# One encoder layer on one NeuronCore: the windowed-attention scores taken two tiles at a time, their low-part product on 64 rows

## The chip, the cores and the metric

The kernel runs on one core of one Trainium2 chip. The metric is the device time of one execution in microseconds (us); where several runs are shown, their median. The engines have short names below: PE is the matrix engine (TensorE), PEld its weight loads, DVE VectorE, ACT ScalarE, POOL GpSimd, and SP the engine that issues the transfers (DMAs).

## The reference, cut to what matters

The layer takes x (2048 tokens, 1024 features) through a LayerNorm, one input projection, three mixers side by side (spatial gating, a depthwise convolution, windowed attention), one output projection, and a last LayerNorm of `alpha*x + y`. The change touches the attention only:

```
s = einsum(q, kb) * HEAD_DIM**-0.5          # 8 query heads of 64, 2 key heads, 4 query heads share one
s = where(|key - query| <= 128, s + bias, -1e30)
m = max(max(s), sink);  p = exp(s - m);  p = p / (sum(p) + exp(sink - m))
o = einsum(p, vb)
```

Everything is computed in float32 quality. PE takes the type fp32r, which keeps fewer bits, so each operand is split into a high part (a rounded copy) and a low part (what the rounding lost), and a product is the sum of partial products of the parts.

## The kernel before, in words

**Stages.** First the input LayerNorm, the transposes of x and the projections of values and keys (to about 130 us). Then 72 steps of the input projection, `feat` (lines 134 to 142): 16 weight blocks in four token chunks of 512 (two more blocks, the last attention gates, make steps 64 to 71), each step 24 matmuls of 512 columns. Beside them run the spatial gating, the convolution on DVE (62 passes over 2048 columns, line 451, spread over steps 8 to 47) and its LayerNorm. From step 67 on the attention is mixed in, and after the last step it runs alone to the end.

**Queries.** Steps 32 to 47 are of kind `cq`. `evac` (line 522) hands the product in PSUM to `split_store` (line 269), which makes the high part on ACT (line 276, with the scale -1/8), the low part on DVE (line 277), and stores them to two DRAM tensors, `qh_d` and `ql_d`. `split_store` serves the keys too (line 290). On DVE the passes of the convolution that belong to a step are tied behind its line 277 through `last[0]` (line 922).

**Keys.** `load_k` (line 561) puts four tiles in SBUF: high and low part of each of the two key heads, each one twice, in partitions 0 to 63 and again in 64 to 127.

**Blocks and slots.** The attention goes by 16 blocks of 128 tokens. `slot(i, h)` (line 816), h from 0 to 7, does a piece of three blocks at once: scores of block i, the probabilities' transposes and value products of block i-1, the output projection of block i-2. On PE the order inside a slot is: the score tile (`scores`, line 686), four transposes (`ptrans`, line 725, in slots 0 to 5 of an inner block), two value matmuls (`pv`, line 735, in slots 2 to 7), six matmuls of the output projection (`oproj`, line 761). Each engine works its instructions in order; the order is set by a scheduler at build time, which follows the program except where it sees an engine waiting.

**One score tile.** At a block's start the query parts are read back into one tile, high part in partitions 0 to 63, low part in 64 to 127 (lines 656, 657), and ACT copies them into `q` with the tokens regrouped (line 660): tile h holds one key head's four query heads for 32 of the 128 tokens, which makes 128 columns. Its window is 288 keys. Two matmuls of 128 rows fill it:

```
for e in range(2):
    T.matmul(ps[:, 0:n], d["q"][:, h, :],
             kt[e * 2 + kv][:, g0:g0 + n], start=(e == 0), stop=(e == 1))
```

The first (e = 0) sums high query times high key and low query times high key; the second high query times low key and low query times low key. DVE then takes the tile out of PSUM, adds the bias and finds the row's extreme (line 697). PSUM tiles of the tag `psD`, of which there are two, hold the scores, and in the projection steps also every other step's `feat` product. In slots 3 and 7 `softmax` (line 702) does the exponentials on ACT (line 710) and the normalisation on POOL (line 719). `finish` (line 796) ends a block with a LayerNorm: POOL's power (line 107), DVE's line 809, two POOL passes.

Of the kernel before, what the change touches and what calls it, by code (L numbers as in the profile page):

```python
# [7 lines left out]
F32 = mybir.dt.float32  # L8
F32R = mybir.dt.float32r
AF = mybir.ActivationFunctionType  # L10
ALU = mybir.AluOpType
# [3 lines left out]
P = 128  # L15
SEQ = 2048
# [3 lines left out]
CH = 512  # L20
# [7 lines left out]
NH = 8  # L28
HD = 64
QS = 32  # L30
WK = 2 * P + QS
# [24 lines left out]
def trunk_kernel(  # L56
# [5 lines left out]
    V, S, G, T, SY = nc.vector, nc.scalar, nc.gpsimd, nc.tensor, nc.sync  # L62
# [4 lines left out]
    def f32(ap):  # L67
        return ap.bitcast(F32)

    constp = tc.alloc_tile_pool(name="constp", bufs=1)  # L70
    dram = tc.alloc_tile_pool(name="dramp", bufs=1, space=DRAM)
# [3 lines left out]
    spo_d = dram.tile([SEQ, 256], F32, name="spo_d")  # L75
    yh_d = dram.tile([4, P, SEQ], F32, name="yh_d")
    yl_d = dram.tile([4, P, SEQ], F32, name="yl_d")
    qh_d = dram.tile([NH * HD, SEQ], F32, name="qh_d")
    ql_d = dram.tile([NH * HD, SEQ], F32, name="ql_d")
    kh_d = dram.tile([P, SEQ], F32, name="kh_d")  # L80
    kl_d = dram.tile([P, SEQ], F32, name="kl_d")
    v_d = dram.tile([NT, P, 2, 2, HD], F32, name="v_d")
# [15 lines left out]
    p_ln = tc.alloc_tile_pool(name="p_ln", bufs=2, side="right", reuse_waits="tile")  # L98
    psp = tc.alloc_tile_pool(name="psp", bufs=2, space=PSUM)
# [46 lines left out]
    last = [None]  # L146
# [29 lines left out]
    for hf in range(2):  # L176
        for a, dst in ((0, grow), (1, brow)):
            ps = psp.tile([P, CH], F32, tag=("psD", "psE")[a], name=f"row{a}_{hf}")
# [87 lines left out]
        V.tensor_tensor(out=vt[:, :, 1, :], in0=src, in1=f32(vt[:, :, 0, :]), op=ALU.subtract)  # L266
        SY.dma_start(v_d[t].rearrange("p a l d -> p (a l d)"), f32(vt).rearrange("p a l d -> p (a l d)"))

    def split_store(ps, hd, ld, scale, pool, bufs, n=CH):
        hi = pool.tile([P, n], F32R, tag="shi", name="shi", bufs=bufs)  # L270
        lo = pool.tile([P, n], F32R, tag="slo", name="slo", bufs=bufs)
        if scale is None:
            S.copy(hi, ps)
            V.tensor_tensor(out=lo, in0=ps, in1=f32(hi), op=ALU.subtract)
        else:
            S.activation(hi, ps, AF.Copy, scale=scale)
            last[0] = V.scalar_tensor_tensor(out=lo, in0=ps, scalar=scale, in1=f32(hi),
                                             op0=ALU.mult, op1=ALU.subtract).ins
        SY.dma_start(hd, f32(hi))
        SY.dma_start(ld, f32(lo))  # L280

    def keys(c, o, n):
        ps = psp.tile([P, n], F32, tag="psD", name=f"ck{c}_{o}")
        for k in range(NK):
            T.matmul(ps, ckh[:, k, :], xc[c][:, 0, k, o:o + n], start=(k == 0), stop=False)
            T.matmul(ps, ckh[:, k, :], xc[c][:, 1, k, o:o + n], start=False, stop=False)
        for k in range(NK):
            T.matmul(ps, ckl[:, k, :], xc[c][:, 0, k, o:o + n], start=False, stop=(k == NK - 1))
        ts = slice(c * CH + o, c * CH + o + n)
        split_store(ps, kh_d[:, ts], kl_d[:, ts], None, p_ln, 1, n)  # L290

    plan = [(BB, "bb", 0), (BA, "ba", 0), (BB + P, "bb", 1), (BA + P, "ba", 1),
            (AU, "au", 0), (AG, "ag", 0), (AU + P, "au", 1), (AG + P, "ag", 1)]
# [13 lines left out]
    for t in range(NT + LOOK):  # L307
# [26 lines left out]
        if u == 4:  # L334
            keys(0, 256, 256)
# [6 lines left out]
    pm = tc.alloc_tile_pool(name="pm", bufs=2, side="right", reuse_waits="tile")  # L342
# [179 lines left out]
    def evac(kind, a, c, ps):  # L522
        cs = slice(c * CH, (c + 1) * CH)
        ps_cs = slice(PAD + c * CH, PAD + (c + 1) * CH)
        if kind == "bb":
            if c == 0:
                g_ = pm.tile([P, SEQ + 2 * PAD + 2], F32, tag="glu", name=f"glu{a}")
                V.memset(g_[:, 0:PAD], 0.0)
                V.memset(g_[:, PAD + SEQ:SEQ + 2 * PAD], 0.0)
                glu.append(g_)  # L530
            S.activation(glu[a][:, ps_cs], ps, AF.Sigmoid)
        elif kind == "ba":
            last[0] = V.tensor_tensor(out=glu[a][:, ps_cs], in0=ps, in1=glu[a][:, ps_cs], op=ALU.mult).ins
            if c == NC - 1:
                avail[0] += KW
        elif kind == "au":
            tm = pm.tile([P, CH], F32, tag="tmp", name=f"gu{a}_{c}")
            S.activation(tm, ps, AF.Gelu_apprx_tanh)
            pt = spt.pop((a, c))
            last[0] = V.tensor_tensor(out=tm, in0=pt, in1=tm, op=ALU.mult).ins  # L540
            ug[a, c] = tm
        elif kind == "cq":
            fs = slice(a * P, (a + 1) * P)
            split_store(ps, qh_d[fs, cs], ql_d[fs, cs], -(HD ** -0.5), pm, 2)
        else:
            tm = pm.tile([P, CH], F32, tag="tmp", name=f"{kind}{a}_{c}")
            S.activation(tm, ps, AF.Silu)  # L547
            if kind == "ag":
                up = ug.pop((a, c))
                last[0] = V.tensor_tensor(out=up, in0=tm, in1=up, op=ALU.mult).ins  # L550
                store_y(a, c, up)
            elif kind == "bg":
                G.tensor_tensor(out=tm, in0=tm, in1=ybt[a][:, cs], op=ALU.mult)
                store_y(2 + a, c, tm)
            else:
                SY.dma_start(g_d[a * P:(a + 1) * P, cs], tm)


    kt = []
# [9 lines left out]
    ar = {}  # L569
    sink = constp.tile([P, NH], F32, name="sink")  # L570
    nsink = constp.tile([P, NH], F32, name="nsink")
# [72 lines left out]
    def load_v(i):  # L644
        SY.dma_start(f32(ar["v"][i % 8]), v_d[i].rearrange("p a l d -> p a (l d)"))

    def rng(i):
        return max(i - 1, 0), min(i + 2, NT)
# [4 lines left out]
    def start_block(i):  # L653
        raw = ar["q"][i % 2]
        cs = slice(i * P, (i + 1) * P)
        SY.dma_start(raw[0:HD], qh_d.rearrange("(h d) t -> d h t", d=HD)[:, :, cs])
        SY.dma_start(raw[HD:P], ql_d.rearrange("(h d) t -> d h t", d=HD)[:, :, cs])
        q = wsp.tile([P, NH, P], F32R, tag="whi", name=f"q{i}")
        for kv in range(2):
            S.copy(q[:, kv * 4:kv * 4 + 4, :].rearrange("p j (r t) -> p j r t", t=QS),  # L660
                   raw[:, kv * 4:kv * 4 + 4, :].rearrange("p r (j t) -> p j r t", t=QS))
        d = {"q": q, "p": [], "pt": {}}
        for nm in "egl":
            d[nm] = pm.tile([P, NH], F32, tag="sm" + nm, name=f"sm{nm}{i}")
        st[i] = d
# [15 lines left out]
    def window(i, j):  # L681

        return (max(QS * j, P) if i == 0 else QS * j,
                min(QS * j + WK, 2 * P) if i == NT - 1 else QS * j + WK)

    def scores(i, h):
        d = st[i]
        kv, j = h // 4, h % 4
        k0, k1 = window(i, j)
        n, b0 = k1 - k0, k0 - QS * j  # L690
        g0 = (i - 1) * P + k0
        ps = psp.tile([P, WK], F32, tag="psD", name=f"s{i}_{h}")
        for e in range(2):
            T.matmul(ps[:, 0:n], d["q"][:, h, :],  # L694
                     kt[e * 2 + kv][:, g0:g0 + n], start=(e == 0), stop=(e == 1))
        s = ar["s"][(i * 2 + kv) % 3 * 4 + j]
        V.tensor_tensor_reduce(out=s[:, k0:k1], in0=ps[:, 0:n], in1=ar["bias"][:, kv, b0:b0 + n],  # L697
                               scale=1.0, scalar=nsink[:, h:h + 1], op0=ALU.add, op1=ALU.min,
                               accum_out=d["g"][:, h:h + 1])
        d["p"].append(s)  # L700

    def softmax(i, kv):
        d = st[i]
# [112 lines left out]
    def slot(i, h):  # L816


        a, b, c = i, i - 1, i - 2
        if h == 0:  # L820
            if a < NT:
                start_block(a)
                if a >= 1 and a + 1 < NT:
                    load_v(a + 1)
            if 0 <= b < NT:
                load_mix(b)
        groups = []
        if 0 <= b < NT:
            lo, hi = rng(b)
            groups = [(kv, j) for kv in range(2) for j in range(hi - lo)]  # L830
        if a < NT:
            scores(a, h)
            if h % 4 == 3:
                softmax(a, h // 4)
        if h < len(groups):
            ptrans(b, *groups[h])
        if 2 <= h < len(groups) + 2:
            pv(b, *groups[h - 2])
        if c == 0:
            oproj(0, 0, h)  # L840
        if c == 1 and h < 2:
            for k in range(4 * h, 4 * h + 4):
                oproj(0, 1, k)
            if h == 1:
                finish(0)
        if c == NT - 1:
            if h < 4:
                oproj(c, 0, 2 * h)
                oproj(c, 0, 2 * h + 1)
            elif h % 2 == 0:  # L850
                oproj_last(c, h // 2 - 2)
        elif 0 < c < NT:
            hf, k = (h // 2) % 2, (h // 4) * 4 + (h % 2) * 2
            oproj(c, hf, k)
            oproj(c, hf, k + 1)
        if h == NH - 1:
            if 0 <= b < NT:
                gate(b)
            if 0 < c < NT:
                finish(c)  # L860
# [33 lines left out]
    for s, (n, c) in enumerate(steps):  # L894
# [16 lines left out]
        ps = feat(wts[n], c, f"{n}_{c}", tag="psE" if s > 11 and kind != "bg" and s % 2 else "psD")  # L911
# [66 lines left out]
```

## Time and profile before

| | |
|---|---|
| Median of 3 runs | 864.47 us (861.98 to 865.37) |
| The profiled execution: its time / its span | 863.25 us / 861.4 us |
| Busy share of PE, PEld, DVE, ACT, POOL | 96%, 82%, 67%, 41%, 31% |
| Granted PE clock, mean | 0.994 |

A timeline row reads: start in us, duration in us, engine, line, operation, output and inputs by the program's names, rows x columns, how many in a row; in brackets the idle time of that engine in front of it and what ended it. Matmuls are pipelined: one's recorded duration (0.39 us at 512 columns) is longer than its turn on the engine, so turns are read from one start to the next. In the chain of waits each piece has only the time that it adds to the chain.

### The profile page before, as it was taken

To read this page: it belongs to the slowest core of one execution; us is meant where nothing else is said; L and a number is where in the kernel's file an instruction comes from. 1 tells how busy PE (TensorE), PEld (TensorE's weight loads), DVE (VectorE), ACT (ScalarE), POOL (GpSimd) and SP (SyncE) were. 2 spreads that over 40 slices of the span, in tenths; PEclk is the share of its full clock that TensorE was granted. 3 is DMA by queue.
4 is the path that set the end of the run, shared out by engine and by line. 5 is a ranking of instruction groups with operands and counts; after the bars stand their busy time and mean duration, and the time that the engine had idled before them with its cause. 6 is when DMAs were issued, how large, how long until landed. Compare 5 with 4: busy or idle time off the path is not lost.

```text
span 861.4 us, 11898 instructions
## 1 busy us (share of the span) xinstructions
PE 830.8 (96%) x4156; PEld 705.6 (82%) x4156; DVE 574.9 (67%) x1012; ACT 352.3 (41%) x764; POOL 270.8 (31%) x320
## 2 busy tenths in 40 slices
PE   6899999999999999999899999999999999999996
PEld 6799987778888888888688887887888888888875
DVE  4888912575779888989642102676788877777764
ACT  3544321332144341122223214865555656565540
POOL 1332410330000000001233320115566655666654
PEclk9999999999999999999999999999999999999999
DMA  8577433232122224378755668987544554442221
GB/s 292 175 242 245 175 130 93 87 98 86 37 74 98 85 74 138 125 250 258 240 188 146 194 189 197 297 309 161 153 116 117 142 150 131 116 117 86 86 95 53
DMA packets 115800, 130.19 MB, mean 151 GB/s; under 512 B 8868, under 2 KB 87251, under 8 KB 115196
## 3 DMA queue, kind: packets, MB, share of 16 engines
q1 hardware_dynamic: 115740, 129.43, 48.9%
q8 instruction: 33, 0.54, 0.3%
q14 instruction: 27, 0.22, 0.1%
HBM read 74.86 MB, written 55.07 MB: 151 GB/s over the span
## 4 chain that ended last, share of the span: by engine, by line
PE 74%; DVE 8%; POOL 6%; DMA 4%; issue 3%; ACT 2%; SPq 1%; POOLq 0%; DVEq 0%; ACTq 0%
PE ft L139 13%; PE ft L140 13%; PE ft L141 13%; PE out L772 4%; PE out L773 4%; PE out L774 4%; PE pt L727 3%; PE s L694 3%; PE av L255 3%; PE av L256 3%; PE av L258 2%; PE pv L744 2%; PE pv L745 2%; POOL arena L719 2%; PE xT L242 2%
## 5 line engine op out<-in xcount | busy, mean ns | idle before, releaser
L139 PE MATMUL ft<-xc,hi_f 128*128 128x512 f32 x576 | 226.5, 393 | 0.0
L141 PE MATMUL ft<-xc,lo_f 128*128 128x512 f32 x576 | 224.5, 390 | 0.0
L140 PE MATMUL ft<-xc,hi_f 128*128 128x512 f32 x576 | 224.4, 390 | 0.0
L451 DVE SCALAR_TENSOR_TENSOR acc<-glu,cw,acc 128x2048 f32<-128x2048 f32 x60 | 140.8, 2346 | 0.6
L141 PEld LDWEIGHTS ft<-xc,lo_f 128*128 128x128 f32 x576 | 108.1, 188 | 22.6
L139 PEld LDWEIGHTS ft<-xc,hi_f 128*128 128x128 f32 x576 | 108.2, 188 | 22.1 <-ACT so L436 0.2
L140 PEld LDWEIGHTS ft<-xc,hi_f 128*128 128x128 f32 x576 | 108.2, 188 | 21.5
L131 POOL TENSOR_TENSOR lo_f<-raw_f,hi_f 128x1024 fp32r<-128x1024 f32 x8 | 21.3, 2659 | 239.5 <-ACT hi_f L129 229.7
L710 ACT ACTIVATE arena<-arena,smg 128x288 f32<-128x288 f32 (+4 forms) x128 | 67.5, 528 | 56.7 <-DVE smg L697 55.6
L697 DVE CUSTOM_DVE_ANT_0 arena<-s,arena,nsink 128x288 f32<-128x288 f32 (+4 forms) x128 | 62.7, 492 | 37.8 <-DMA arena<-qh_d 19.3
L732 DVE TENSOR_TENSOR arena<-pt,arena 128x512 fp32r<-128x512 f32 x92 | 62.8, 685 | 14.8 <-ACT arena L731 14.6
L731 ACT CAST arena<-pt 128x512 fp32r<-128x512 f32 x92 | 53.2, 582 | 33.0 <-PE pt L727 32.4
L727 PE MATMUL pt<-ident,arena 128*128 128x128 f32 x368 | 56.1, 274 | 4.9 <-DVE arena L732 4.9
L757 POOL TENSOR_TENSOR arena<-arena,gt 128x512 f32<-128x512 f32 x16 | 20.7, 1296 | 121.0 <-DVE arena L750 73.2
L694 PEld LDWEIGHTS s<-k,q 128*128 128x128 f32 x256 | 46.8, 188 | 12.9 <-DVE smg L697 1.5
L694 PE MATMUL s<-k,q 128*128 128x288 f32 (+4 forms) x256 | 54.5, 297 | 1.3 <-ACT cg L547 0.7
L719 POOL TENSOR_SCALAR arena<-arena,sml 128x288 f32<-128x288 f32 (+2 forms) x104 | 50.1, 500 | 6.3 <-ACT bot L748 3.9
L772 PE MATMUL out<-wo,yh 128*128 128x512 f32 x124 | 52.0, 419 | 0.0
L727 PEld LDWEIGHTS pt<-ident,arena 128*128 128x128 f32 x368 | 44.1, 140 | 8.7 <-issue 4.4
L773 PE MATMUL out<-wo,yh 128*128 128x512 f32 x124 | 49.3, 397 | 0.0
L774 PE MATMUL out<-wo,yl 128*128 128x512 f32 x124 | 48.8, 394 | 0.0
L772 PE MATMUL out<-wo,arena 128*128 128x512 f32 x124 | 48.7, 392 | 0.0
(184 smaller groups left out, 1534.9 us busy)
## 6 DMA issues: line engine op xcount, KB each, us to landing
raw_f<-in_w_in_dram SPq DMA_DIRECT2D x18, 512.0 KB, 4.5
xhat_d<-x SPq DMA_DIRECT2D x16, 512.0 KB, 4.6
r<-xhat_d SPq DMA_DIRECT2D x16, 512.0 KB, 3.9
x<-in_x_dram SPq DMA_DIRECT2D x15, 512.0 KB, 3.9
out_dram<-r SPq DMA_DIRECT2D x15, 512.0 KB, 3.1
yh_d<-shi SPq DMA_DIRECT2D x16, 256.0 KB, 2.1
yl_d<-slo SPq DMA_DIRECT2D x16, 256.0 KB, 2.4
qh_d<-shi SPq DMA_DIRECT2D x16, 256.0 KB, 2.2
```

Source lines behind the costliest of these rows:

```text
L139: T.matmul(ps, hi[:, k, :], xh, start=(k == 0), stop=False)
L140: T.matmul(ps, hi[:, k, :], xl, start=False, stop=False)
L141: T.matmul(ps, lo[:, k, :], xh, start=False, stop=(k == NK - 1))
L451: V.scalar_tensor_tensor(out=acc[a], in0=glu[a][:, k:k + SEQ], scalar=cw[:, a, k:k + 1], in1=acc[a], op0=ALU.mult, op1=ALU.add)
L694: T.matmul(ps[:, 0:n], d["q"][:, h, :], kt[e * 2 + kv][:, g0:g0 + n], start=(e == 0), stop=(e == 1))
L710: S.activation(p, p, AF.Exp, bias=d["g"][:, h:h + 1], scale=-1.0, accum_out=d["l"][:, h:h + 1])
L719: (V if i < 3 else G).tensor_scalar(out=p, in0=p, scalar1=d["l"][:, h:h + 1], scalar2=1.0, op0=ALU.mult, op1=ALU.mult)
L727: T.transpose(ps[:, r, :], d["p"][kv * 4 + r][:, f0:f0 + P], ident)
L732: V.tensor_tensor(out=pl, in0=pf, in1=f32(ph), op=ALU.subtract)
L772: T.matmul(ps, hi, wh, start=(k == 0), stop=False)
L773: T.matmul(ps, hi, wl, start=False, stop=False)
L774: T.matmul(ps, lo, wh, start=False, stop=(k == NK - 1))
```

## The change

The two DRAM tensors of the queries no longer hold high and low part apart. By 32-token groups they alternate: `qa_d` holds the high part of even groups and the low part of odd groups, `qb_d` the rest. After the read-back an even tile has its high part in partitions 0 to 63, an odd tile in 64 to 127. Scores are then taken for two tiles at once, in even slots only. Each tile keeps its first matmul on 128 rows; the second is cut to the 64 rows of the high part, times the same rows of the keys' low part, so that the even tile uses the array's upper half and the odd tile its lower half. The product of the two low parts falls away.

```diff
-    def split_store(ps, hd, ld, scale, pool, bufs, n=CH):
+    def split_store(ps, hd, ld, pool, bufs, n=CH):
...
+    def query_store(ps, ad, bd):
+        a = pm.tile([P, CH], F32R, tag="shi", name="qa")
+        b = pm.tile([P, CH], F32R, tag="slo", name="qb")
+        scale = -(HD ** -0.5)
+        src, av, bv = (v.rearrange("p (j e t) -> p j e t", e=2, t=QS) for v in (ps, a, b))
+        for e, hi in ((0, av), (1, bv)):
+            S.activation(hi[:, :, e, :], src[:, :, e, :], AF.Copy, scale=scale)
+        for e, hi, lo in ((0, av, bv), (1, bv, av)):
+            last[0] = V.scalar_tensor_tensor(out=lo[:, :, e, :], in0=src[:, :, e, :], scalar=scale,
+                                             in1=f32(hi[:, :, e, :]), op0=ALU.mult, op1=ALU.subtract).ins
+        SY.dma_start(ad, f32(a))
+        SY.dma_start(bd, f32(b))
...
     def scores(i, h):
         d = st[i]
...
-        for e in range(2):
-            T.matmul(ps[:, 0:n], d["q"][:, h, :],
-                     kt[e * 2 + kv][:, g0:g0 + n], start=(e == 0), stop=(e == 1))
...
+        ws = [window(i, h % 4 + e) for e in range(2)]
+        pss = [psp.tile([P, WK], F32, tag="psD", name=f"s{i}_{h + e}") for e in range(2)]
+        for l in range(2):
+            for e, (k0, k1) in enumerate(ws):
+                g0 = (i - 1) * P + k0
+                rows = slice(0, P) if l == 0 else slice(e * HD, (e + 1) * HD)
+                T.matmul(pss[e][:, 0:k1 - k0], d["q"][rows, h + e, :],
+                         kt[l * 2 + kv][rows, g0:g0 + k1 - k0], start=(l == 0), stop=(l == 1))
+        for e, (k0, k1) in enumerate(ws):
...
+            V.tensor_tensor_reduce(out=s[:, k0:k1], in0=ps[:, 0:n], in1=ar["bias"][:, kv, b0:b0 + n],
...
         if a < NT:
-            scores(a, h)
+            if h % 2 == 0:
+                scores(a, h)
             if h % 4 == 3:
                 softmax(a, h // 4)
```

The number of transfers and their sizes stay, and so do the number of matmuls (four for two tiles) and the number of evacuations (line 697).

## Rows read from the trace of the kernel before

**Rows 1.** The page: busy time of PE, and the chain's share by engine.

```profile
PE 830.8 (96%) x4156; PEld 705.6 (82%) x4156; DVE 574.9 (67%) x1012; ACT 352.3 (41%) x764; POOL 270.8 (31%) x320
...
PE 74%; DVE 8%; POOL 6%; DMA 4%; issue 3%; ACT 2%; SPq 1%; POOLq 0%; DVEq 0%; ACTq 0%
```

**Rows 2.** Stages of the attention: us, busy of PE, PEld, DVE, ACT, POOL; clock, DMA.

```profile
560.00:600.00 40.00, 40.00 (x213) 33.75 (x211) 30.20 (x76) 22.51 (x55) 13.31 (x15) 1.00 0.83 247
600.00:830.00 230.00, 225.67 (x1193) 191.95 (x1193) 176.88 (x431) 133.40 (x349) 143.00 (x169) 0.99 0.43 122
```

**Rows 3.** The chain of waits, one inner block: start, us added, engine and line.

```profile
711.83 0.59 ACT bot L748
...
714.01 0.40 DVE arena L697
...
718.63 0.81 DVE r L809
...
720.19 0.63 PE pt L727 x4
```

**Rows 4.** Waits between 600 and 820 us: total us, times, longest.

```profile
PE pt L727 <- DVE arena L732: 4.3, 12, 2.1
```

**Rows 5.** Timeline of one slot of an inner block.

```profile
703.30 0.39 PE L774 MATMUL out<-wo,yl 128*128 128x512 f32 x1
...
703.53 0.43 PE L694 MATMUL s<-k,q 128*128 128x288 f32 x2
703.67 0.49 PEld L727 LDWEIGHTS pt<-ident,arena 128*128 128x128 f32 x4
703.80 0.60 PE L727 MATMUL pt<-ident,arena 128*128 128x128 f32 x4
704.13 0.19 PEld L744 LDWEIGHTS pv<-arena 128*128 128x128 f32 x1
...
704.24 0.19 PEld L745 LDWEIGHTS pv<-arena 128*128 128x128 f32 x1
```

**Rows 6.** Timeline around the two 31-row transposes of line 370.

```profile
144.65 0.39 PE L141 MATMUL ft<-xc,lo_f 128*128 128x512 f32 x1
...
144.97 0.19 PEld L370 LDWEIGHTS ps_cw<-ident,cwr 31*128 31x128 f32 x2 [0.35 <-issue]
144.97 0.30 PE L370 MATMUL ps_cw<-ident,cwr 31*128 31x31 f32 x2
...
145.20 0.19 PEld L139 LDWEIGHTS ft<-xc,hi_f 128*128 128x128 f32 x1
...
145.31 0.19 PEld L140 LDWEIGHTS ft<-xc,hi_f 128*128 128x128 f32 x1
```

**Rows 7.** Timeline around the 33-row product of line 351.

```profile
138.32 0.39 PE L141 MATMUL ft<-xc,lo_f 128*128 128x512 f32 x1
138.63 0.09 PEld L351 LDWEIGHTS ps_tb<-hot,rb 33*8 33x8 f32 x2 [0.35 <-DVE gw L122]
...
139.07 0.59 PE L351 MATMUL ps_tb<-hot,rb 33*8 33x512 f32 x1
...
139.59 0.42 PEld L394 LDWEIGHTS ps_wt<-ident,wsr 128*128 128x128 f32 x4 [0.86 <-issue]
...
139.64 0.14 PEld L394 LDWEIGHTS ps_wt<-ident,wsr 128*128 128x128 f32 x1
```

**Rows 8.** Splits by line and shape, ACT and DVE: busy us, mean ns, idle before.

```profile
L276 ACT ACTIVATE shi<-ft 128x512 fp32r<-128x512 f32 x16 | 9.6, 598 | 48.9 <-PE ft L141 48.9
...
L273 ACT CAST shi<-ck 128x256 fp32r<-128x256 f32 x2 | 0.7, 373 | 2.8 <-PE ck L288 2.8
...
L277 DVE SCALAR_TENSOR_TENSOR slo<-ft,shi 128x512 fp32r<-128x512 f32 x16 | 11.0, 685 | 4.5 <-ACT shi L276 2.6 <-DMA ql_d<-slo 1.9
...
L274 DVE TENSOR_TENSOR slo<-ck,shi 128x256 fp32r<-128x256 f32 x2 | 0.8, 418 | 0.0
```

**Rows 9.** Waits between 300 and 530 us: PE at the end of the convolution.

```profile
PE cl L472 <- DVE acc L451: 2.8, 1, 2.8
```

More of the change, by code (lines that the diff above doesn't have):

```diff
@@ L77, in trunk_kernel @@
     yl_d = dram.tile([4, P, SEQ], F32, name="yl_d")
-    qh_d = dram.tile([NH * HD, SEQ], F32, name="qh_d")
-    ql_d = dram.tile([NH * HD, SEQ], F32, name="ql_d")
+    qa_d = dram.tile([NH * HD, SEQ], F32, name="qa_d")
+    qb_d = dram.tile([NH * HD, SEQ], F32, name="qb_d")
     kh_d = dram.tile([P, SEQ], F32, name="kh_d")
@@ L267, in av_tile @@
         SY.dma_start(v_d[t].rearrange("p a l d -> p (a l d)"), f32(vt).rearrange("p a l d -> p (a l d)"))
-    def split_store(ps, hd, ld, scale, pool, bufs, n=CH):
+    def split_store(ps, hd, ld, pool, bufs, n=CH):
         hi = pool.tile([P, n], F32R, tag="shi", name="shi", bufs=bufs)
         lo = pool.tile([P, n], F32R, tag="slo", name="slo", bufs=bufs)
[L272 to L278, printed above, removed]
+        S.copy(hi, ps)
+        V.tensor_tensor(out=lo, in0=ps, in1=f32(hi), op=ALU.subtract)
         SY.dma_start(hd, f32(hi))
         SY.dma_start(ld, f32(lo))
+    def query_store(ps, ad, bd):
[10 more added lines that the diff above has]
+        SY.dma_start(bd, f32(b))
     def keys(c, o, n):
@@ L289, in keys @@
         ts = slice(c * CH + o, c * CH + o + n)
-        split_store(ps, kh_d[:, ts], kl_d[:, ts], None, p_ln, 1, n)
+        split_store(ps, kh_d[:, ts], kl_d[:, ts], p_ln, 1, n)
     plan = [(BB, "bb", 0), (BA, "ba", 0), (BB + P, "bb", 1), (BA + P, "ba", 1),
@@ L543, in evac @@
             fs = slice(a * P, (a + 1) * P)
-            split_store(ps, qh_d[fs, cs], ql_d[fs, cs], -(HD ** -0.5), pm, 2)
+            query_store(ps, qa_d[fs, cs], qb_d[fs, cs])
         else:
@@ L655, in start_block @@
         cs = slice(i * P, (i + 1) * P)
-        SY.dma_start(raw[0:HD], qh_d.rearrange("(h d) t -> d h t", d=HD)[:, :, cs])
-        SY.dma_start(raw[HD:P], ql_d.rearrange("(h d) t -> d h t", d=HD)[:, :, cs])
+        SY.dma_start(raw[0:HD], qa_d.rearrange("(h d) t -> d h t", d=HD)[:, :, cs])
+        SY.dma_start(raw[HD:P], qb_d.rearrange("(h d) t -> d h t", d=HD)[:, :, cs])
         q = wsp.tile([P, NH, P], F32R, tag="whi", name=f"q{i}")
@@ L687, in scores @@
         d = st[i]
[L688 to L692, printed above, removed]
-        for e in range(2):
-            T.matmul(ps[:, 0:n], d["q"][:, h, :],
-                     kt[e * 2 + kv][:, g0:g0 + n], start=(e == 0), stop=(e == 1))
[L696 to L700, printed above, removed]
+        kv = h // 4
+        ws = [window(i, h % 4 + e) for e in range(2)]
[7 more added lines that the diff above has]
+        for e, (k0, k1) in enumerate(ws):
+            j, n, ps = h % 4 + e, k1 - k0, pss[e]
+            b0 = k0 - QS * j
+            s = ar["s"][(i * 2 + kv) % 3 * 4 + j]
+            V.tensor_tensor_reduce(out=s[:, k0:k1], in0=ps[:, 0:n], in1=ar["bias"][:, kv, b0:b0 + n],
+                                   scale=1.0, scalar=nsink[:, h + e:h + e + 1], op0=ALU.add, op1=ALU.min,
+                                   accum_out=d["g"][:, h + e:h + e + 1])
+            d["p"].append(s)
     def softmax(i, kv):
```

## The prediction

> **What bounds the kernel now.** I read the page first: PE is busy for 96% of the span and makes 74% of the chain that ended last, with DVE next at 8% [rows 1]. Then the table by stage, since an average says little about the attention, where the change lies: PE is busy for all of 560 to 600 us and for 225.67 of the next 230 us, at a granted clock of 0.99 to 1.00 [rows 2]. So from 560 us on nearly each tenth of a microsecond added to PE's turn is added to the end, and one taken off is a gain only if no other chain stands close behind. The chain of waits shows that one does. In an inner block of 19 us it leaves PE at the block's last value product, goes over ACT's copy (711.83), DVE's evacuations (714.01), POOL and DVE's line 809 (718.63), and comes back to PE at the transposes of slot 3 (720.19) [rows 3]. These wait 12 times between 600 and 820 us, 4.3 us in all with one long one of 2.1: the other eleven wait 0.2 us each [rows 4]. Last I read a slot in the timeline, for turns: 512 columns take 0.23 us (703.30 to 703.53), the two score matmuls 0.27 together (703.53 to 703.80), that is 0.133 each [rows 5].
>
> **How loads hide.** The load of the transposes' weights starts at 703.67, where the second score matmul begins its turn: a load runs under the matmul in front of it. What a load takes is seen where two meet: 704.13 to 704.24, 0.11 us for a matmul's weights [rows 5]. So 0.133 of a score matmul hides its successor's 0.11.
>
> **What the change does on PE.** Two tiles now take four turns of 0.133, 0.53 us. After it there are two of 128 rows (A0, A1) and two of 64 (B0, B1), and no matmul or load is fewer. Whatever is gained must come from B0 and B1 running beside each other. What is lost depends on the array's change from 128 rows to 64 and back, which the trace has twice in near form. Before the 31-row transposes the load doesn't start under the matmul in front, at 144.65, but 0.32 us later at 144.97, and the row says that it waited for nothing ("issue"); that is 0.09 after the matmul's 0.23 turn. Behind them the next 128-row load starts at 145.20, not under them, and its matmul when it is done, at 145.31 (where the following load starts) [rows 6]. Before and behind the 33-row product it is the same: a load 0.31 us after the start of the matmul in front (the row names a DVE instruction here, so this one could be a wait for data), and behind it the load at 139.59, 0.52 after the start of the second product at 139.07. A product's own turn there is some 0.43 (from just behind the load at 138.63 to 139.07), so this is again 0.09 past the end, and again "issue" [rows 7]. I read these as one thing: a matmul of fewer rows waits until the array has run empty, and so does the first full one after it; 0.09 us each way, and the load that was hidden comes on top.
>
> No row has 64 rows, only 31 and 33. The Trainium skill, TensorEngine Tiling (Array Packing), Tiling Modes, lists 64 rows as a mode of its own and says that changing the mode, not just the tile, drains the engine; the rows agree for 31 and 33 rows, and by the rule 64 pays the same.
>
> **The sum for a pair.** Into 64 rows: 0.09 wait and 0.11 load, 0.20. B0 and B1: with loads one behind the other, B1 starts 0.11 after B0 and takes its 0.13: 0.24 where two turns took 0.27, so 0.03 gained. Back to 128 rows: 0.09 and the next load. In slots 0, 2 and 4 transposes follow, whose first load on an empty array took 0.05 (139.59 to 139.64 [rows 7]): 0.14. In slot 6 a value product follows: 0.09 + 0.11 = 0.20. A pair thus costs 0.20 - 0.03 + 0.14 = 0.31 more, in slot 6 0.37. With 16 blocks: 48 x 0.31 + 16 x 0.37 = 20.8 us. Bounds from the same rows: at best both switches are free and B1 lies wholly under B0, -0.133 a pair or -8.5 us; at worst a switch stands between B0 and B1 too, +0.22 a pair, +35 us in all. I take 20.8, because the rows nearest in kind show both switches.
>
> **What hides some of it.** The pairs of slots 0 and 2 put 0.62 us more between the last value product and the transposes of slot 3, so the eleven waits of 0.2 go: -2.2 us.
>
> **The other parts.**
> - Query splits: one ACT pass of 598 ns becomes two of 256 columns, by the nearest row 373 each, +0.15 us; on DVE 685 becomes 2 x 418, +0.15 [rows 8]. Over 16 steps 2.4 us on each. ACT is 41% busy and PE waits for none of it; PSUM is freed 0.3 us later in a step of 24 turns. DVE's part pushes the convolution, whose end PE awaits for 2.8 us [rows 9]: between 0 and 2.4, I take 1.2, as nothing excludes either end.
> - Evacuations come in twos. The second stands ahead of DVE's other work by 0.40 [rows 3], in the slots where PE is 0.31 later anyway; I cost it at nothing. Without that cover it would be 0.4 in the 12 waiting blocks, 5 us.
> - A pair takes both buffers of its PSUM tag. The pair before was evacuated a slot earlier, so A1 waits for nothing; if DVE is late, all of PE is queued behind A1. In the mixed steps the projection uses the same tag: some ten pairs, at most one evacuation each, 0 to 4 us; I take 0, since PE's order there is the scheduler's.
> - The odd tile's exponentials can begin a slot earlier, and the block's `q` comes free earlier. Both feed the chain of [rows 3], which is off the path once PE is slower: 0.
> - Transfers keep their number, size and queue: 0. Key loads are untouched.
>
> **Sum:** 20.8 - 2.2 + 1.2 = 19.8. The profiled execution took 863.25 us, 1.85 more than its span of 861.4 and 1.2 less than the median of the runs. 863.25 + 19.8 = 883.1, in terms of the median 884.
>
> **Rivals.**
> 1. *Both loads side by side* (0.12). If the two halves load at once, B1 starts with B0: 0.11 less a pair, 7 us, 877. For it: they use different rows. Against: every load in the rows follows another. The Trainium skill, TensorE: Matmul & The Clock Gate, Part 3, puts tiles in different row groups some 4 ns apart, which by itself would make this sum 877 too; no row before shows two row groups.
> 2. *A switch between the halves too* (0.12). B0's turn, 0.20, B1's turn: 0.46 in place of 0.24, +14 us, 898. For it: the lower half is another place in the array. Against: the two 31-row transposes follow each other within 0.30 us in all, without a wait, though in the same place [rows 6].
> 3. *No switch, the gain arrives* (0.11), the other side. 64 rows are then fed like 128, B0's load lies under A1, and B1 runs beside B0: 64 x 0.133 = 8.5 us off PE. The chain of [rows 3] does not get shorter, so the pairs of slots 0 and 2 in the eleven waiting blocks give back up to 11 x 2 x 0.133 = 2.9; with 1.2 for the splits it is 4.4 to 7.3 us faster, 857 to 860. What decides is where B0's load starts: at A1's start this case, 0.09 behind its turn mine. For it: only 31 and 33 rows are shown waiting, few times, at odd data. Against: for two of those four waits the row names no other cause, and the other two are as long.
> 4. *It does nothing* (0.10). No switch, but the halves take turns, 0.53 as before: only the splits remain, 865 to 867.
>
> **How the numbers follow.** The forecast has 0.55; its own range is 877 to 891 (exit loads up or down by 0.05 a pair, the idle time absorbed from 0 to 4.3, splits 0 to 2.4, some us of PSUM waits). With rivals 1 and 2 it makes 0.79 slower. A measurement of this kernel can tell about 0.5%, 4.3 us, from no change: rival 4 is within it (0.10) with a little of rival 3 (0.01), and the rest of rival 3, 0.10, is faster. The range from 868 to 899 holds the forecast and rivals 1 and 2 and what lies between 1 and 4; it leaves out rival 3 and most of 4.
>
> **What would show it.** Right: the load of B0 stands some 0.22 us behind A1's start instead of at it; from A0's start to the next instruction's start about 0.85 us; the granted clock still near 1; an inner block of some 20 us instead of 19; the 0.2 us waits of slot 3 gone. B1's start 0.11 behind B0's confirms serial loads, at once is rival 1, 0.33 is rival 2. Wrong: B0's load under A1 (rivals 3 and 4), or PE idle at A1 for PSUM, or PE waiting for the end of the convolution much longer than 2.8 us.

## The result, and the profile after

Before 865.09 us (median of 6 runs, 861.98 to 866.16), after 876.18 us (6 runs, 874.67 to 879.43): slower by 1.4%, ratio 1.0138 [1.0122, 1.0155]. The medians differ by 11.1 us, the spans of the two profiled executions by 12.8 (861.4 and 874.2). The forecast was 884, its range 868 to 899.

The page of the changed kernel, busy time and the chain's shares, beside [rows 1]:

```profile
PE 848.2 (97%) x4156; PEld 701.5 (80%) x4156; DVE 585.8 (67%) x1028; ACT 348.7 (40%) x780; POOL 270.7 (31%) x320
...
PE 73%; DVE 9%; POOL 5%; ACT 4%; DMA 4%; issue 3%; SPq 0%; POOLq 0%; DVEq 0%; ACTq 0%
```

PE has as many matmuls as before and is busy 17 us longer, so they take longer turns. The table by stage (us, busy of PE, PEld, DVE, ACT, POOL; clock) says where, beside [rows 2]:

```profile
560.00:600.00 40.00, 40.00 (x198) 31.66 (x199) 31.20 (x76) 24.72 (x63) 11.58 (x11) 1.00 0.82 236
600.00:830.00 230.00, 229.25 (x1168) 180.59 (x1166) 179.36 (x418) 124.14 (x337) 141.06 (x164) 1.00 0.43 121
```

The attention now has no gap on PE: 229.25 of 230 us where it was 225.67, at a granted clock of 1.00 (2.4 GHz) where it was 0.99. Fewer matmuls stand in the same 230 us (1168 for 1193). An inner block takes 19.8 us (700.44 to 720.23, the starts of two like pairs) where it took 19.0.

The timeline of two pairs, in slot 0 (PE and its loads) and in slot 6, to be read against [rows 5]:

```profile
700.44 0.76 PE L708 MATMUL s<-k,q 128*128 128x288 f32 x4
700.80 0.19 PEld L708 LDWEIGHTS s<-k,q 64*128 64x128 f32 x2 [0.17 <-issue]
701.13 0.42 PEld L744 LDWEIGHTS pt<-ident,arena 128*128 128x128 f32 x4
701.14 0.66 PE L744 MATMUL pt<-ident,arena 128*128 128x128 f32 x4
...
715.74 0.76 PE L708 MATMUL s<-k,q 128*128 128x288 f32 x4
716.10 0.19 PEld L708 LDWEIGHTS s<-k,q 64*128 64x128 f32 x2 [0.17 <-issue]
716.43 0.19 PEld L761 LDWEIGHTS pv<-arena 128*128 128x128 f32 x1
716.54 0.19 PEld L762 LDWEIGHTS pv<-arena 128*128 128x128 f32 x1
```

Three things are to be seen. The 64-row loads do not start under A1, which took its turn from 700.58 (one 0.14 turn behind 700.44), but 0.22 later, and the row says "issue". Both loads together last 0.19, as long as one alone does: so they start at the same instant. And the next 128-row load starts 0.33 behind them instead of under a matmul. The four transposes then begin at 701.14 and take 0.66 instead of 0.60, so full work resumes at 701.20: 0.76 for two tiles where two single tiles took 0.53. In slot 6 the value product takes its turn when its load is done and the following one starts, 716.54: 0.80.

The waits between 600 and 820 us (total us, times, longest), first one line of the kernel before, then the changed kernel's, and PE's at the end of the convolution, beside [rows 4] and [rows 9]:

```profile
ACT arena L758 <- POOL arena L757: 11.5, 11, 1.5
```

```profile
ACT arena L775 <- POOL arena L774: 34.9, 11, 3.3
...
PEld s L708 <- issue: 7.3, 44, 0.2
...
PEld pt L744 <- DVE arena L749: 1.5, 7, 0.2
```

```profile
PE cl L482 <- DVE acc L461: 2.9, 1, 2.9
```

The 4.3 us in which PE's transposes waited for DVE are gone; what is left is 1.5 on the load sequence. A query split is now two passes of 256 columns on ACT and two on DVE (some 380 and 417 ns each in the groups by shape, for 598 and 685 in [rows 8]), and PE's wait for the convolution's end has not grown (2.8 before). One line is new in size: ACT waits 34.9 us for POOL's gate product, 3.2 a block, where it waited 11.5 in the kernel before. Nothing on PE waits behind it here, but the experiments show what it is.

### The profile page after: what moved, and what is told of

It is laid out like the page before. It is cut to its first block, busy times and chain, and to the rows that moved or that the text cites. A ratio compares the mean times of both kernels' runs of the same rounds, so it can differ in the third digit from the quotient of the medians.

```text
span 874.2 us, 11954 instructions
## 1 busy us (share of the span) xinstructions
PE 848.2 (97%) x4156; PEld 701.5 (80%) x4156; DVE 585.8 (67%) x1028; ACT 348.7 (40%) x780; POOL 270.7 (31%) x320
## 4 chain that ended last, share of the span: by engine, by line
PE 73%; DVE 9%; POOL 5%; ACT 4%; DMA 4%; issue 3%; SPq 0%; POOLq 0%; DVEq 0%; ACTq 0%
PE ft L139 12%; PE ft L141 12%; PE ft L140 12%; PE out L789 4%; PE out L790 4%; PE out L791 4%; PE pt L744 3%; PE s L708 3%; PE av L255 3%; PE av L256 3%; PE av L258 2%; PE xT L242 2%; PE pv L761 2%; PE pv L762 1%; DVE acc L461 1%
## 5 line engine op out<-in xcount | busy, mean ns | idle before, releaser
L461 DVE SCALAR_TENSOR_TENSOR acc<-glu,cw,acc 128x2048 f32<-128x2048 f32 x60 | 142.8, 2381 | 0.6
L749 DVE TENSOR_TENSOR arena<-pt,arena 128x512 fp32r<-128x512 f32 x92 | 62.6, 683 | 35.1 <-ACT arena L748 35.1
L714 DVE CUSTOM_DVE_ANT_0 arena<-s,arena,nsink 128x288 f32<-128x288 f32 (+4 forms) x128 | 60.5, 501 | 33.2 <-PE s L708 33.2
L736 POOL TENSOR_SCALAR arena<-arena,sml 128x288 f32<-128x288 f32 (+2 forms) x104 | 50.4, 505 | 76.5 <-ACT bot L765 49.0
L744 PE MATMUL pt<-ident,arena 128*128 128x128 f32 x368 | 58.0, 280 | 2.0 <-DVE arena L749 2.0
L748 ACT CAST arena<-pt 128x512 fp32r<-128x512 f32 x92 | 52.7, 576 | 7.3 <-PE pt L744 6.6
L744 PEld LDWEIGHTS pt<-ident,arena 128*128 128x128 f32 x368 | 41.5, 140 | 17.3 <-DVE arena L749 4.1
L708 PE MATMUL s<-k,q 128*128 128x288 f32 (+5 forms) x256 | 51.3, 345 | 0.3
L708 PEld LDWEIGHTS s<-k,q 128*128 128x128 f32 (+1 forms) x256 | 36.7, 185 | 17.9 <-issue 9.9
L789 PE MATMUL out<-wo,arena 128*128 128x512 f32 x124 | 48.7, 393 | 0.0
L790 PE MATMUL out<-wo,arena 128*128 128x512 f32 x124 | 48.6, 392 | 0.0
```

The lines of the kernel that those rows point to most:

```text
L461: V.scalar_tensor_tensor(out=acc[a], in0=glu[a][:, k:k + SEQ], scalar=cw[:, a, k:k + 1], in1=acc[a], op0=ALU.mult, op1=ALU.add)
L708: T.matmul(pss[e][:, 0:k1 - k0], d["q"][rows, h + e, :], kt[l * 2 + kv][rows, g0:g0 + k1 - k0], start=(l == 0), stop=(l == 1))
L744: T.transpose(ps[:, r, :], d["p"][kv * 4 + r][:, f0:f0 + P], ident)
L749: V.tensor_tensor(out=pl, in0=pf, in1=f32(ph), op=ALU.subtract)
L789: T.matmul(ps, hi, wh, start=(k == 0), stop=False)
L790: T.matmul(ps, hi, wl, start=False, stop=False)
```

## The experiments

In the list, "ratio" is to the kernel before on the same chip; its medians there are 862.92 to 864.15 us, so the experiments are compared by their ratios. The first theory was the prediction's: the loss is the turn from 128 rows to 64 and back. Its rivals: that it is the pairing itself (two tiles in one slot), or the query splits.

**e1_pair_128rows.** The changed kernel, its second product on all 128 rows.

```diff
-                rows = slice(0, P) if l == 0 else slice(e * HD, (e + 1) * HD)
+                rows = slice(0, P)
```

> The changed kernel with the second product of each tile on all 128 rows again; tiles still in pairs, queries still split the new way. Theory (the loss is the array's change to 64 rows and back, 0.22 to 0.27 us a pair): the loss goes, 863 to 867 us beside some 865 of the kernel before, and the load of the third score matmul stands at the start of the second one. Rival A (the pairing itself costs: two evacuations in a row, both PSUM tiles at once): stays at 873 to 877. Rival B (the query splits cost): between 867 and 870.

872.42 us, ratio 1.0107 [1.0090, 1.0124]. No turn to 64 rows is left, and three quarters of the loss is. The theory that the turn alone is the loss fell here; the time lies just under the range of rival A, that the pairing costs. The table by stage, the waits of 600 to 820 us and the chain of one block show a bound of another kind:

```profile
680.00:720.00 40.00, 38.44 (x205) 31.97 (x204) 30.97 (x72) 21.79 (x60) 24.19 (x29) 1.00 0.46 126
```

```profile
ACT arena L775 <- POOL arena L774: 38.8, 12, 3.2
...
PE pt L744 <- DVE arena L749: 8.0, 11, 0.8
```

```profile
716.25 1.47 POOL arena L736 x3
717.73 1.27 POOL arena L774
719.02 0.63 ACT arena L775
719.66 0.60 ACT arena L748
720.28 0.70 DVE arena L749
721.03 0.66 PE pt L744 x4
```

PE idles 1.6 of 40 us, and its transposes wait 0.7 in each of eleven blocks. From the bottom up: the transposes wait for DVE, whose subtraction (L749) is the last to read an earlier group of transposes; it needs ACT's copy of them (L748); that stands in ACT's queue behind the gate's copy (L775), and that waits for POOL's gate product (L774), which stands behind POOL's normalisations (L736). In the kernel before, POOL does four normalisations, the gate product, then the other four; in both paired kernels all eight come first. I read it so: the odd tile's scores are there a slot earlier, so the scheduler can put the second head's normalisations earlier, and the gate comes behind them. The gate's input is ready at 716.50 (line 767's end), and the product starts 1.2 us later.

**e2_single_64rows.** The kernel before, with the second product of each single tile on rows 0 to 63: the turn without the pairing.

```diff
-            T.matmul(ps[:, 0:n], d["q"][:, h, :],
-                     kt[e * 2 + kv][:, g0:g0 + n], start=(e == 0), stop=(e == 1))
+            rows = slice(0, P) if e == 0 else slice(0, 64)
+            T.matmul(ps[:, 0:n], d["q"][rows, h, :],
+                     kt[e * 2 + kv][rows, g0:g0 + n], start=(e == 0), stop=(e == 1))
```

> The kernel before, tile by tile, but the second product of every tile on the upper 64 rows alone (the product of the two low parts is left out). Theory: each of the 128 tiles pays the way to 64 rows and back, 0.34 us more where transposes follow and 0.39 where a value product follows: 16 x (6 x 0.34 + 2 x 0.39) = 45, less some 2 of idle time: about 906 to 910 us. Rival A (pairing is the cost): as before, 865. If a 64-row matmul cost nothing but its turn: 865.

901.36 us, ratio 1.0446 [1.0427, 1.0465]. Timeline of one tile, and a stage:

```profile
720.73 0.62 PE L695 MATMUL s<-k,q 128*128 128x288 f32 x2
...
720.95 0.18 PEld L695 LDWEIGHTS s<-k,q 64*128 64x128 f32 x1 [0.26 <-issue]
721.28 0.42 PEld L728 LDWEIGHTS pt<-ident,arena 128*128 128x128 f32 x4
```

```profile
680.00:720.00 40.00, 40.00 (x188) 29.81 (x187) 29.11 (x71) 21.02 (x55) 22.15 (x26) 1.00 0.41 117
```

The load comes 0.22 behind the tile's start and the next one 0.33 behind that, as in the pair; with the transposes' 0.06 a tile takes 0.61 for 0.27, and 0.65 where a value product follows. 16 x (6 x 0.34 + 2 x 0.38) is 44.8 us; less the 4.3 of [rows 4] that PE no longer waits, 40.5. Measured: 38.4, below the 906 to 910 expected, which had taken off only 2 for idle time; some 2 us stay unexplained. PE is busy in all of every window. So the price of a turn is as the prediction built it, and it is paid nearly in full when nothing else is in the way.

**e3_pair_same_half.** Pairs in the old layout, both 64-row products on the upper half of the array. The edit is e1's `scores` with

```diff
+                rows = slice(0, P) if l == 0 else slice(0, HD)
```

> Pairs as in the changed kernel, but with the old query layout, so that both 64-row products sit on the upper half (product of the two low parts left out). Theory that two different halves load and run side by side: here B1's load comes 0.11 us behind B0's and its turn behind B0's turn, 0.11 to 0.13 more a pair than the changed kernel, 7 to 8.5 us: 883 to 885. Rival (loads on an empty array overlap whatever the rows): 876, like the changed kernel.

880.63 us, ratio 1.0202 [1.0185, 1.0220]. The loads and the pair:

```profile
708.38 0.89 PE L698 MATMUL s<-k,q 128*128 128x288 f32 x4
708.73 0.29 PEld L698 LDWEIGHTS s<-k,q 64*128 64x128 f32 x2 [0.17 <-issue]
709.19 0.42 PEld L734 LDWEIGHTS pt<-ident,arena 128*128 128x128 f32 x4 [0.16 <-issue]
```

Two loads now last 0.29, so the second starts 0.10 to 0.11 behind the first, and the next full load 0.46 behind them, not 0.33. In this timeline the two halves are worth 0.12 (the transposes' load comes 0.81 behind the pair's start, not 0.69) to 0.13 of a pair, as expected. The whole kernels differ by less: 0.64% of the time, 5.5 us, which is 0.09 a pair and less than the 7 to 8.5 expected. No switch stands between two products in one half. The change's idea works as far as this; it is the way in and out that costs more.

**e4_single_96rows.** As e2, with rows 0 to 95.

> The kernel before, tile by tile, but the second product on rows 0 to 95 (a quarter of the contraction, half of the product of the two low parts, is left out). Theory (what costs is that the array is set to another size, 64 rows and not 96): about as before, 864 to 867 us, loads hidden under the matmul in front. Rival (any matmul with fewer rows than the one in front waits for the array to run empty): some 906 to 910, like the 64-row run.

863.93 us, ratio 0.9996 [0.9981, 1.0011]. The tile and its second load:

```profile
701.93 0.19 PEld L695 LDWEIGHTS s<-k,q 96*128 96x128 f32 x1
...
701.92 0.43 PE L695 MATMUL s<-k,q 128*128 128x288 f32 x2
...
704.82 0.43 PE L695 MATMUL s<-k,q 128*128 128x288 f32 x2
705.09 0.60 PE L728 MATMUL pt<-ident,arena 128*128 128x128 f32 x4
```

The load starts with the tile, under its first matmul. The way back is free too: a slot later (704.82) the transposes start 0.27 behind the tile, as before. Fewer than 128 rows is not what costs: 96 rows are free here, 64 (and 33 and 31, [rows 6, 7]) are not.

**e5_pair_old_split.** e1 with the queries split and stored as in the kernel before.

```diff
-            query_store(ps, qa_d[fs, cs], qb_d[fs, cs])
+            split_store(ps, qh_d[fs, cs], ql_d[fs, cs], -(HD ** -0.5), pm, 2)
```

> Pairs, the second product on 128 rows, and the old query split (one pass on ACT, one on DVE): what is left of the change is the pairing alone. Theory: 862 to 866 us, within 2 us of the run with the new split. If the splits cost (Rival B): that run is 3 or more above this one. If the pairing costs (Rival A): 873 to 877 here too.

873.24 us, ratio 1.0121 [1.0103, 1.0140], beside e1's 1.0107 [1.0090, 1.0124]: no difference beyond the noise, and inside the range of rival A. The splits cost nothing that can be measured.

**e6_pair_one_left_out.** e1 without the odd tile's second product: a stand-in for the gain that the change could have at best, a turn less in each pair and no turn to 64 rows.

```diff
+                if l == 1 and e == 1:
+                    continue
```

> Pairs on 128 rows with the odd tile's second product left out (that tile lacks query high part times key low part): what the change would bring if the two 64-row products ran wholly side by side and nothing were paid for it. One turn of 0.133 us less a pair, 8.5 us on PE. Theory: PE bounds, but the chain over ACT, DVE and POOL stands 0.2 us behind it in each block and gives some back: 857 to 861. If that chain binds as tightly as PE: 862 to 865.

871.15 us, ratio 1.0081 [1.0058, 1.0105]; PE's wait:

```profile
PE pt L746 <- DVE arena L751: 13.8, 11, 1.8
```

Both expected ranges are missed. PE is busy 5.5 us less than in e1 (827.3 and 832.8 us on the two pages), and yet both profiled spans are 869.6 us: the wait at the transposes takes it up, 13.8 us where e1 has 8.0. By the ratios e6 is 0.3% below e1, with intervals that overlap, so at most some 2 of the 8.5 us may have arrived. In a paired kernel whose queues stand like this, even a free second product would not have made it faster than before.

**e11_before_gate_last.** Meant as the test of e1's explanation the other way round: the kernel before, unpaired, with POOL's gate product tied behind the normalisations.

```diff
+        if 2 <= i < NT - 1:
+            with tc.issue_after(normed_p[0]):
+                product()
```

> The kernel before, tile by tile, with POOL's product of the gate forced behind the second head's normalisations, the order that the pairing brought. Theory: this alone costs most of what pairing costs, 868 to 874 us. Rival (the order hurts only with pairs): 862 to 866.

872.72 us, ratio 1.0098 [1.0072, 1.0124]. PE's wait at the transposes, and POOL and DVE at the end of a block:

```profile
PE pt L730 <- DVE arena L735: 10.3, 12, 0.9
```

```profile
722.98 1.29 POOL L768 TENSOR_TENSOR arena<-arena,arena 128x512 fp32r<-128x512 f32 x1
...
723.05 1.77 DVE L818 TENSOR_SCALAR r<-r,nsm,nsr 128x1024 f32<-128x1024 f32 x1 [2.25 <-POOL nsr L107]
```

The time is the expected one, a loss of 9 us with no pair in the kernel, but it does not come by e1's chain. With the edit a second POOL instruction changed its place: the gate's subtraction (L768), which in the kernel before and in e1 comes ahead of POOL's power (L107), now comes behind it (722.98, the power at 722.47). There DVE's pass of the LayerNorm (L818, line 809 of the kernel before) runs beside it, and it takes 1.77 us in all eleven blocks; in the kernel before it takes 0.81 ([rows 3]), and in e1 0.81 too. This pass is a link of the chain of [rows 3], and it accounts for the loss: the power starts 0.26 earlier behind the end of `bot` than before (5.38 and 5.64 us), the pass takes 0.96 longer, and a block is 0.70 longer (19.68 from one `bot` to the next, 18.98 before). So e11 shows that an order on POOL can cost 1%. It does not show that the place of the gate's product is what costs e1 its time.

**e7_pair_gate_first, e8_change_gate_first, e9_left_out_gate_first.** e5, the changed kernel and e6, each with POOL's gate product tied ahead of the second head's normalisations again, as in the kernel before.

```diff
+            if a < NT:
+                if a >= 3:
+                    with tc.issue_after(gated[0]):
+                        normalise(a, 1)
```

> As e5 (pairs, 128 rows, old split), with one order put back: POOL multiplies the gate in (line 757 of the kernel before) ahead of the second head's four normalisations, as it did in the kernel before; the build's scheduler had turned this round in every paired kernel. Theory now (the pairing costs by this order on POOL: ACT's copy of the gated block waits for it, and behind it ACT's evacuation of the transposes): back to 861 to 866 us, POOL-to-ACT wait of 3 us a block gone. Rival (it is the evacuations in twos on DVE, or the PSUM tiles): stays at 871 to 875.

> The changed kernel with the same order put back on POOL. Theory (in the changed kernel two limits stand at almost the same height, the order on POOL and PE's 0.22 to 0.27 us a pair for the change to 64 rows): PE holds it, a block of some 19.7 us stays: 873 to 877, slower than before by 1.0 to 1.5%. Rival (the switch costs little, the order made nearly all of the loss): 863 to 868.

> As e6 (pairs on 128 rows, the odd tile's second product left out: one turn of 0.133 us less a pair) with the order put back on POOL: the gain that the change could have had without the array's switch. Theory: 856 to 861, as first expected of e6. If another chain still binds: 862 to 866.

873.83 us (ratio 1.0110 [1.0086, 1.0133]), 876.50 (1.0142 [1.0119, 1.0165]) and 872.15 (1.0095 [1.0072, 1.0117]): each as without the edit. e7 goes with its rival, e8 with its theory (PE is busy for 229.12 of the 230 us from 600 on), and e9 misses both its ranges. In e7's timeline POOL's order is back, the product at 719.04 and the normalisations behind it, and that alone gives nothing back. e7's wait; the timeline of ACT at a block's end, with PE's last value product; from the chain of waits the transposes that follow; and that product in the kernel before:

```profile
PE pt L738 <- DVE arena L743: 10.7, 11, 1.0
```

```profile
716.24 0.39 PE L756 MATMUL pv<-arena 128*128 128x512 f32 x1
...
716.32 0.54 ACT L718 ACTIVATE arena<-arena,smg 128x288 f32<-128x288 f32 x1 [0.75 <-DVE smg L705]
...
716.86 0.52 ACT L718 ACTIVATE arena<-arena,smg 128x288 f32<-128x288 f32 x1
...
717.43 0.21 ACT L720 ACTIVATE sme<-sme 128x4 f32<-128x4 f32 x1
717.66 0.58 ACT L759 COPY bot<-pv 64x512 f32<-64x512 f32 x1
```

```profile
726.03 0.63 PE pt L738 x4
```

```profile
711.23 0.39 PE L745 MATMUL pv<-arena 128*128 128x512 f32 x1
```

The copy `bot` heads the chain of [rows 3] (there at 711.83). PE's last value product of that head starts at 716.24 and ends its turn 0.23 later, but `bot` starts at 717.66, 1.19 us behind that end, after the last exponential and the sink's. In the kernel before these two come after it, and it starts 0.37 behind the product's end (711.23 and its turn). From `bot` to the transposes that wait the chain is as long as before: 8.37 us here (to 726.03), 8.36 there (711.83 to 720.19). So the 0.82 us by which `bot` is late is all of the 0.83 by which e7's block is longer (19.81 from one `bot` to the next, 18.98 before). `bot` is as late in e1 (1.20 us), so there two queues were late, and e7 set one of them right. I read it as the odd tile again: evacuated with its neighbour, its exponential is ready sooner and stands earlier in the queue, ahead of work that PE waits for.

**e12_pair_queues_as_before, e13_change_queues_as_before.** The last two: e7's orders, and with them `bot` ahead of the last exponential on ACT, the gate's subtraction behind the normalisations on POOL, and the odd tile evacuated a slot later, as before. e12 with 128 rows, e13 the change itself.

```diff
+            elif a >= 3:
+                with tc.issue_after(turned_p[0]):
+                    scored(a, h, 1)
...
+        if kv and i >= 3:
+            with tc.issue_after(boted[0]):
+                rest()
```

> Pairs with the second product on all 128 rows, as in e7, and now the queues of the three other engines stand as in the kernel before: POOL has the gate's product ahead of the second head's normalisations and the gate's subtraction behind them, ACT has the copy of the second head's lower half ahead of the last score tile's exponential and the sink's, and DVE evacuates the odd tile a slot later, behind the subtraction of that slot's transposes (but not tile 7, which is still evacuated with tile 6). If what pairing costs is the order in those queues, about all of e7's 10 us goes: 862 to 867, PE back above 39.5 of 40 us in each window, and no wait of PE's transposes for DVE above 0.3 us on average. If pairing costs something on PE itself, or the other order that is left (tile 7's evacuation with tile 6's) is the cost, 871 to 875 as in e5 and e7. In between would mean that the orders explain a part.

> The change itself (second product on 64 rows) with the same orders on POOL, ACT and DVE as e12. The prediction's theory is that the turns into and out of 64 rows are paid on PE whatever stands in the other queues: sixteen... fourteen blocks of some four pairs at 0.22 to 0.27 each, 14 to 15 us for all 64 pairs, less the short waits of PE that they swallow (2.2), so 873 to 878, and PE at 39.9 of 40 us or more in every window. The rival, that the queue orders make the time of the changed kernel and the turns lie beside them: it falls to 862 to 868 with e12.

875.78 us, ratio 1.0136 [1.0114, 1.0158], and 881.56 us, ratio 1.0201 [1.0178, 1.0223]. Both miss both expectations, e12 by 0.8 us above its rival's 871 to 875: nothing is given back. e13 is worse than e8; e12 lies above e7, but their intervals overlap. e12's waits and the timeline at one of them:

```profile
PEld s L699 <- DVE smg L712: 12.5, 22, 0.8
...
PE s L699 <- DVE smg L712: 5.1, 11, 0.5
```

```profile
713.94 0.29 PE L699 MATMUL s<-k,q 128*128 128x288 f32 x1
...
714.13 0.50 DVE L712 CUSTOM_DVE_ANT_0 arena<-s,arena,nsink 128x288 f32<-128x288 f32 x1
...
714.69 0.30 PEld L699 LDWEIGHTS s<-k,q 128*128 128x128 f32 x2 [0.78 <-DVE smg L712]
714.69 0.40 PE L699 MATMUL s<-k,q 128*128 128x288 f32 x1 [0.45 <-DVE smg L712]
```

`bot` is no longer late: it starts 0.19 us behind its product. The transposes' waits for DVE are gone from the list, and PE waits at the scores instead: A0 starts at 713.94, A1 not before 714.69, when DVE has emptied the odd tile of the pair before. A pair takes both PSUM buffers, so an odd tile that is evacuated late holds up the next pair, and one that is evacuated early stands, as e1 and e7 are read here, ahead of other work in the queues. In e13 this wait is added to the turns: PE is busy 39.53 of 40 us there, not 39.98, and the time is 5 us above the change's. So PE's wait stood in three places in turn (DVE behind ACT behind POOL; ACT's `bot`; PSUM), and the time of pairs on 128 rows stayed at 871 to 876. e12 changed three orders at once, and one of them brought the new wait. The run that puts only `bot` ahead, with the odd tile still evacuated early, was not made, and a third score buffer was not tried: whether either would free pairs of their cost is open.

## Why the prediction was right, and where it was not

**Right: the sign and the mechanism on PE.** The 64-row load stands 0.22 behind A1's start (forecast "some 0.22"), the clock stays at 1.00, a block is 19.8 us instead of 19 (forecast "some 20"), and the 0.2 waits of slot 3 are gone. The rule of the Trainium skill that the prediction weighed (TensorEngine Tiling (Array Packing), Tiling Modes: a change of the mode drains the engine) agrees with the trace here for 64 rows, 0.34 a tile in e2. e4's free 96 rows agree with it too, if they count as the full mode.

**Mis-sized: B1 behind B0.** The sum had 0.31 a pair (0.37 in slot 6); the rows give 0.76 - 0.53 = 0.23 and 0.80 - 0.53 = 0.27. The step that failed is "with loads one behind the other, B1 starts 0.11 after B0": the loads start together. That is rival 1's mechanism, and e3 shows the alternative, 0.10 to 0.11 apart in one half. The sign that went with the forecast, some 0.85 us from A0 to the next instruction, came out at 0.70 to the transposes' start and 0.76 to full work. The sum on PE is 48 x 0.23 + 16 x 0.27 = 15.4 us, not 20.8.

**Mis-sized: what is absorbed.** Eleven waits of 0.2 were taken off, 2.2; the twelfth, the long one of 2.1 in [rows 4], went too. With 4.3 the sum is 15.4 - 4.3 = 11.1, beside a measured 11.1 by the medians; with an uncertainty of some 1.4 us in the ratio, and of 0.01 in each start, that the two agree to a tenth is chance. The two profiled executions differ by 12.8 us: by the pages PE is busy 17.4 longer and idle 4.6 less. The range's own terms (0 to 4.3) held this.

**Mis-sized: the splits.** 1.2 in the sum; e5 shows no cost, and PE's wait behind the convolution went from 2.8 to 2.9.

**Wrong as a mechanism: "evacuations come in twos ... I cost it at nothing" and "the odd tile's exponentials can begin a slot earlier ... 0".** The cover named was that PE is slower anyway. In the changed kernel this holds: PE has no gap, so the queues' delays lie beside the turns, and the two do not add. But by themselves they cost 9.5 us (e1), nearly as much as the turns, and twice the 5 us named for the lost cover. Had someone made only the pairing, the same working would have said "no change" and been wrong. The price was sought in DVE's 0.4 us an evacuation; by the timelines it lay in the order in which other queues stand after an early result. One row of the chain before gave a hint of this. The prediction has the chain leave PE at the last value product and go to `bot`; it leaves PE at a score tile and goes first over ACT's copy of the queries:

```profile
710.88 0.28 PE s L694 x2
...
711.18 0.62 ACT q L660
```

`bot` stood in ACT's queue even before, 0.37 us behind its product, and whatever more is put ahead of it there lengthens that chain.

**Rivals.** Rival 1 was right in its mechanism (877 against 876.2). Rival 2's switch between halves is absent: both loads start at once. Rival 3, the gain that arrives, fell twice: the load doesn't lie under A1, and in e6 most of a turn less per pair did not arrive, since PE then waits for the longer chain; the 2.9 us of give-back that it allowed were far too few. Rival 4 fell with the timeline.

**What is shown and what is argued.** Shown: the turn's price (e2), the gain of two halves (e3), that pairing alone costs 1.1% (e1, e5), that an order on POOL can cost 1.0%, by a slower DVE pass that no paired kernel has (e11), and that putting POOL's order back doesn't cure a pair (e7). Argued from the timelines only: that the place of POOL's gate product holds PE in e1, and that ACT's `bot` holds it in e7; there the times add up, but no run moved `bot` alone. No version here beats the kernel before.

## What to carry to other kernels

Before a matmul is cut to part of the array's rows, look in the timeline at where the next load starts: a load that lay under its predecessor and no longer does costs more than the saved turn when the matmul is as short as 0.13 us; several 64-row products between one way in and one way out might pay, a single pair doesn't. Where one engine has no gap, price a regrouping by what it does to the order of the other queues as well, and undo each half of a change alone: here two losses of about one per cent lay side by side, and either alone would have looked like the whole cause. When a queue is set right and the time stays, ask which buffer or queue is late next. And when a run meets its expected time, see in its timeline that it does so by the expected chain: e11 did not.

## What the runs showed of the hardware that was not expected

Two 64-row loads for different halves of the array start at the same instant (x2 in 0.19 us); for the same half they stand 0.10 to 0.11 apart (x2 in 0.29 us). A 96-row matmul between 128-row ones waits for nothing, its load starting 0.01 us behind the tile's start, while a 64-row one makes a tile of 0.27 us take 0.61. A DVE pass over 128x1024 float32 that takes 0.81 us in the other kernels takes 1.77 in e11, in all eleven blocks, where a POOL subtraction of 1.29 us starts just ahead of it (L818 and L768); by this e11's block is longer.
